# First modulation round in two halves of the features, and the first two SGU tiles begun on the first half

## The chip, the cores and the metric

The kernel runs on one core of a Trainium2 chip, as one program. The metric is the device time of one execution in microseconds (us), shorter is better. The engines are TensorE (PE; PEld is its weight load), VectorE (DVE), ScalarE (ACT), GpSimd (POOL) and SyncE (SP), which mostly issues DMAs. Each engine works through its own instructions in a fixed order and waits on semaphores for the others.

## What is computed

One step of a small hybrid decoder: 1024 prompt tokens and 8 samples of one token each (1032 columns in the kernel), 1024 features. There are two layers. The token mixer of layer 0 is a spatial gating unit (SGU), that of layer 1 sparse attention; a gated ConvGLU follows each. Every sub-layer is modulated by the conditioning vector c:

```python
def ada_params(c, w_ada, b_ada):
    return (jax.nn.silu(c) @ w_ada + b_ada).reshape(c.shape[0], N_MOD, D_MODEL)
def modulate(x, shift, scale):
    return x * (1 + scale[:, None, :]) + shift[:, None, :]
...
        hp = modulate(xp, mp[:, 0], mp[:, 1])
...
def sgu_mixer(h, w_in, b_in, norm_g, norm_b, w_s, b_s, w_out):
    z = jax.nn.gelu(h @ w_in + b_in)
    u, v = jnp.split(z, 2, axis=-1)
```

The change touches only the beginning: shift and scale of layer 0's first sub-layer (the first 2048 of 6144 columns of `w_ada[0]`), `h`, and the first two of sixteen 128-column tiles of `h @ w_in`.

## The kernel before

Activations lie feature-major: a feature tile k (0 to 7) is 128 partitions, the tokens are columns, in three chunks c of 384, 384 and 264 (`CH`; the last 8 columns are the samples). Products are made to float32 accuracy from pieces in a reduced format: every operand is split into a high and a low part, `Hh` and `Hl` for the input, `whi` and `wlo` for the weights, and `mm3` multiplies high by high, high by low and low by high. One `dense` tile is thus 8 x 3 matmuls into one PSUM bank. There are two sets of four banks, `psA` and `psB`.

The start goes like this. `fetch_x` loads rows of x, `turn_x` transposes them on PE and copies them out of PSUM to `R` (ACT for even feature tiles, DVE for odd). `ada_round(0, 0, ...)` loads the first 2048 columns of `w_ada[0]` in eight row blocks k of two 512 KB pieces and multiplies each with silu(c) (L239, L242); its last step copies the sums (L247), transposes them and adds the bias into `MOD` (L255). The bias comes from `PAR`, all small parameters turned feature-major, which `load_params` loads in ten small DMAs (L221) and turns (L228). `affine` makes scales and shifts of `MOD`. `apply` makes `Hh` on ACT (L343), the same in full accuracy as `ht` on DVE (L344), and their difference `Hl` on POOL for even, on DVE for odd feature tiles (L349). `zload` loads one tile of the SGU weights and splits it: on ACT and DVE for tiles 0 and 1 (L101, L106), on POOL for the others (L103, L106). The pool `wp` holds four such parts, so the parts of tile 2 take the place of those of tile 0. `sgu_v(i, c)` is tile i of the gate side over chunk c, with a gelu on ACT (L484); it also scales `R` on POOL (L485).

The order of each engine is not the order of the code: a scheduler of the framework interleaves the instructions by priority and by estimated times when the program is built. DMAs pass through eight completion lanes in turn, over all issuing engines, so the DMA issued as number n waits until number n - 8 has landed. Two steps that belong to later stages were placed into this start by the scheduler: four DMAs that load the page table (L778) and the step of DVE that uses them (L781).

Of the kernel before, what the change touches and what calls it, by code (L numbers as in the profile page):

```python
# [34 lines left out]
# background steps taken per step of the products: indexer, keys and values, queries, attention  # L35
PUMP = (3, 4, 4)
PKV, PQ, PL = 7, 8, 2
# searches for thresholds: which blocks go together on which engine, how many run side by side, steps per step
# [3 lines left out]
# attention: heads in flight by block, units of products ahead of the first block, start of the samples' attention  # L42
# [3 lines left out]
# engines that split the query and output weights  # L46
QE = "GV"
# last feature tiles of each ConvGLU whose down products go by chunks of tokens
KEEP = (3, 4)
# output: columns of the last affine on VectorE, blocks that use the second set of banks  # L50
# [5 lines left out]
def hybrid_step(  # L56
# [51 lines left out]
    def load_w(src, cols, pool=None, eng="GG"):  # L108
        """A [1024, cols] piece of weights, split into two parts."""
# [11 lines left out]
    def load_rows(src, pool=None, eng="GG"):  # L121
        """A [128, 1024] piece of weights."""
# [13 lines left out]
    def load_half(src, j, eng):  # L136
        """Rows 512 j.. of a [1024, 128] piece of weights, both parts in one tile."""
# [46 lines left out]
    def tr(out, in_):  # L184
        PE.transpose(out, in_, ident[:in_.shape[0], :in_.shape[0]])  # L185

    crow = Tt("crow", tag="E")
    SP.dma_start(crow[0:1, :D], c_prompt)
    SP.dma_start(crow[1:9, :D], c_sample)
# [22 lines left out]

    def load_params():
        PROW = Tt("prow", tag="E")
        r = 0
        for src in rows:
            n, s = src.shape[0], 0
            while s < n:
                m = min(n - s, 128 - r % 128)
                i = r // 128  # L220
                SP.dma_start(PROW[r % 128:r % 128 + m, i * 128:(i + 1) * 128], src[s:s + m, :])  # L221
                s += m
                r += m
        b = bank("B")
# [5 lines left out]
    def ada_round(L, r, mk):  # L230
        """w_ada[L][:, 2048 r : 2048 (r+1)] for the nine rows of conditioning, feature-major."""
# [32 lines left out]
    # x, feature-major  # L264
# [22 lines left out]

    win = sgu_w_in[0]
# [11 lines left out]
    # per-feature scales of each sub-layer's input and of its residual  # L300
# [10 lines left out]
    def affine(L, i, lnix):  # L311
        """h = n * G + B and x = n * g + b for n the normalised tokens (or the inputs themselves)."""
# [24 lines left out]
    def apply(c, k, b, af, R, lo="G"):  # L337
        """b: n^T of feature tile k in PSUM (or the inputs), over the tokens of chunk c."""
# [25 lines left out]
    def norm_block(src, j, nt, tag="B"):  # L364
        """Token-major normalised block j; src(k) gives its feature tile k, feature-major."""
# [31 lines left out]
    fetch_x(0)  # L397
    turn_x(0)
    first = ["T"] * 13 + ["P"] * 2 + ["W"]
    steps = ada_round(0, 0, lambda: wp.tile([128, SLOT], F32, name="adaw", tag="W") if first[0] == "W" else Tt("adaw", tag=first.pop(0)))  # L400
    for fn in steps[:8]:
        fn()
    zload(0)
    load_params()
    fetch_x(1)
    fetch_x(2)
    first[:] = ["E"]
    steps[8]()
    af = affine(0, 0, None)

    def first_h(c):
        for k in range(KT):
            apply(c, k, R[c][:, k, :], af, None, "GV"[k % 2])

    first_h(0)
    zload(1)

# [32 lines left out]
    # convolution state of the samples  # L450
# [28 lines left out]
    def sgu_v(i, c):  # L479
        b = dense(pieces[i], 128, c)  # L480
# [4 lines left out]
        G.tensor_scalar(R[c][:, i, :], R[c][:, i, :], ALPHA, 0.0, op0=OP.mult, op1=OP.add)  # L485

    for c in range(3):
        sgu_v(0, c)
        sgu_v(1, c)
        if c < 2:  # L490
            turn_x(c + 1)
            first_h(c + 1)
# [943 lines left out]
```

## Time and profile before

| | |
|---|---|
| median of 3 timed runs | 2643.59 us (2638.25 to 2645.91) |
| profiled execution, span | 2642.5 us (1.1 below that median) |
| PE busy | 2536.9 us, 96% of the span |
| DVE, POOL, ACT busy | 1684.3, 996.0, 793.1 us |
| HBM traffic | 178.41 MB read, 11.27 MB written, 72 GB/s over the span |

The table is read from the top: the span is nearly the timed run, and one engine, PE, fills most of it. The question for any change is then in which stretches PE is not busy, or busy at a lower clock, and what it waits for there. Times of rows count from the span's start.

### The profile page before, as it was taken

Reading aid. Unit: us, or ns where it says so; the run is one execution under the profiler, and the core shown is the slowest. Engines: PE = TensorE matmul, PEld = TensorE weight load, DVE = VectorE, ACT = ScalarE, POOL = GpSimd, SP = SyncE. Lnnn points to the kernel's source line nnn. Section 1 sums busy time; section 2 is a strip of 40 time slices with the busy share of each in tenths; the row PEclk is TensorE's granted clock in tenths of the full one; section 3 lists DMA queues with packets and bytes.
Section 4 is the critical chain, followed back from the end, with each engine's and each line's share of the span. In section 5 each row is a group of like instructions: output and inputs, shape, how many; then the busy total and the mean of one; then the engine's idle time right before and its main releaser. Section 6 shows DMA issues by size and latency. Waiting matters only on the chain.

```text
span 2642.5 us, 40989 instructions
## 1 busy us (share of the span) xinstructions
PE 2536.9 (96%) x15920; PEld 2373.0 (90%) x15920; DVE 1684.3 (64%) x3905; ACT 793.1 (30%) x1610; POOL 996.0 (38%) x1066
## 2 busy tenths in 40 slices
PE   7999999999999999999999989898999999999996
PEld 4898798999999999998887979777999999999996
DVE  3323336677667667755798986434777777777747
ACT  3121224111111111124576876532411111111121
POOL 2433525332222223234245765534523333223335
PEclk8999999999999999999999999998999999999998
DMA  7323402222222222211114112233211111111111
GB/s 274 106 63 106 126 9 72 81 89 80 72 88 87 76 78 91 62 37 50 60 34 117 45 53 64 72 117 108 61 49 48 49 42 44 44 48 48 49 41 66
DMA packets 201928, 192.14 MB, mean 73 GB/s; under 512 B 9806, under 2 KB 178246, under 8 KB 200951
## 3 DMA queue, kind: packets, MB, share of 16 engines
q1 hardware_dynamic: 199047, 180.08, 21.9%
q0 software_dynamic: 2688, 9.44, 1.1%
q8 instruction: 126, 2.06, 0.3%
q14 instruction: 67, 0.55, 0.1%
HBM read 178.41 MB, written 11.27 MB: 72 GB/s over the span
## 4 chain that ended last, share of the span: by engine, by line
PE 77%; DVE 10%; POOL 4%; DMA 4%; ACT 3%; issue 3%; SPq 0%; ACTq 0%; POOLq 0%; DVEq 0%
PE psA L84 48%; PE psB L84 21%; PE psB L185 3%; DVE Cc L655 3%; PE psB L242 2%; DVE R L575 1%; ACT junk L920 1%; PE psA L185 1%; DVE junk L889 1%; DVE S L869 1%; DMA raw<-in_dsa_w_out_dram 1%; DMA adaw<-in_w_ada_dram 1%; DVE R L579 1%; POOL whi L103 1%; DMA pidx<-in_page_table_dram 0%
## 5 line engine op out<-in xcount | busy, mean ns | idle before, releaser
L84 PE MATMUL psA<-Hh,whi 128*128 128x384 f32 (+1 forms) x2912 | 940.2, 324 | 17.3 <-POOL whi L103 8.6
L84 PE MATMUL psA<-Hl,whi 128*128 128x384 f32 (+1 forms) x2912 | 938.5, 322 | 1.0 <-POOL Hl L349 0.7
L84 PE MATMUL psA<-Hh,wlo 128*128 128x384 f32 (+1 forms) x2912 | 936.1, 322 | 1.8 <-DVE wlo L106 1.8
L575 DVE SCALAR_TENSOR_TENSOR R<-psB,g,R 128x384 f32<-128x384 f32 (+1 forms) x952 | 525.6, 568 | 299.1 <-PE psB L84 296.9
L103 POOL TENSOR_SCALAR whi<-raw 128x1024 fp32r<-128x1024 f32 x179 | 194.1, 1084 | 1111.3 <-PE psA L84 978.9
L84 PEld LDWEIGHTS psA<-Hh,whi 128*128 128x128 f32 x2912 | 551.8, 190 | 45.7 <-issue 20.7
L84 PEld LDWEIGHTS psA<-Hl,whi 128*128 128x128 f32 x2912 | 552.6, 190 | 9.8 <-issue 6.7
L84 PEld LDWEIGHTS psA<-Hh,wlo 128*128 128x128 f32 x2912 | 552.1, 190 | 8.0 <-issue 5.0
L106 POOL TENSOR_TENSOR wlo<-raw,whi 128x1024 fp32r<-128x1024 f32 x163 | 402.5, 2469 | 12.7
L84 PE MATMUL psB<-gh,whi 128*128 128x384 f32 (+1 forms) x1056 | 342.7, 325 | 6.0 <-DVE t L578 3.0
L84 PE MATMUL psB<-gh,wlo 128*128 128x384 f32 (+1 forms) x1056 | 338.2, 320 | 0.0
L84 PE MATMUL psB<-gl,whi 128*128 128x384 f32 (+1 forms) x1056 | 337.9, 320 | 0.0
L655 DVE SCALAR_TENSOR_TENSOR Cc<-As,PAR,Cc 128x256 f32<-128x256 f32 (+3 forms) x264 | 270.4, 1024 | 54.9 <-ACT Cc L650 53.7
L84 PEld LDWEIGHTS psB<-gh,whi 128*128 128x128 f32 x1056 | 198.6, 188 | 29.7 <-issue 15.3
L84 PEld LDWEIGHTS psB<-gl,whi 128*128 128x128 f32 x1056 | 198.7, 188 | 0.0
L84 PEld LDWEIGHTS psB<-gh,wlo 128*128 128x128 f32 x1056 | 198.5, 188 | 0.0
L101 ACT ACTIVATE gh<-Cc 128x384 fp32r<-128x384 f32 x132 | 65.0, 492 | 432.7 <-DVE Cc L662 432.7
L657 ACT ACTIVATE Cc<-Cc 128x384 f32<-128x384 f32 x132 | 64.9, 492 | 402.1 <-DVE Cc L655 402.1
L649 ACT ACTIVATE As<-psA 128x384 f32<-128x384 f32 x132 | 60.4, 458 | 342.4 <-PE psA L84 342.4
L84 PE MATMUL psB<-Hh,wh 128*128 128x384 f32 (+1 forms) x512 | 136.2, 336 | 3.2 <-ACT R L351 1.1
L662 DVE TENSOR_TENSOR Cc<-psA,Cc 128x384 f32<-128x384 f32 x132 | 67.7, 513 | 107.6 <-PE psA L84 107.1
L579 DVE TENSOR_TENSOR R<-R,t 128x8 f32<-128x8 f32 x328 | 131.0, 406 | 2.9
(352 smaller groups left out, 3284.1 us busy)
## 6 DMA issues: line engine op xcount, KB each, us to landing
raw<-in_ffn_w_up_dram SPq DMA_DIRECT2D x88, 512.0 KB
raw<-in_w_ada_dram SPq DMA_DIRECT2D x64, 512.0 KB
raw<-in_ffn_w_down_dram SPq DMA_DIRECT2D x44, 512.0 KB
adaw<-in_w_ada_dram SPq DMA_DIRECT2D x32, 512.0 KB
raw<-in_sgu_w_in_dram SPq DMA_DIRECT2D x16, 512.0 KB
raw<-in_dsa_w_in_dram SPq DMA_DIRECT2D x16, 512.0 KB
raw<-in_dsa_w_out_dram SPq DMA_DIRECT2D x32, 256.0 KB
raw<-in_sgu_w_out_dram SPq DMA_DIRECT2D x8, 512.0 KB
```

The costliest lines, as they stand in the source:

```text
L84: PE.matmul(out, l, r, start=start, stop=stop)
L101: A.activation(hi, src, AF.Copy)
L103: G.tensor_scalar(hi, src, 1.0, 0.0, op0=OP.mult, op1=OP.add)
L106: (V if e_lo == "V" else G).tensor_tensor(lo, src, f(hi), op=OP.subtract)
L185: PE.transpose(out, in_, ident[:in_.shape[0], :in_.shape[0]])
L242: PE.matmul(st["b"][32 * g:32 * g + 32, :512], SCT[:, k, :], rw[g // 2][:, (g % 2) * 512:(g % 2 + 1) * 512], start=(k == 0), stop=(k == KT ...
L575: V.scalar_tensor_tensor(R[c][:, dt, :npr], b[:, :npr], gp[:, dt:dt + 1], R[c][:, dt, :npr], op0=OP.mult, op1=OP.add)
L579: V.tensor_tensor(R[c][:, dt, npr:n], R[c][:, dt, npr:n], t8, op=OP.add)
L649: A.activation(As[:, c0:c0 + n], b[:, :n], AF.Copy)
L655: V.scalar_tensor_tensor(Cc[:, a0:c0 + npr], As[:, a0 - d:c0 + npr - d], w, Cc[:, a0:c0 + npr], op0=OP.mult, op1=OP.add)
L657: A.activation(Cc[:, c0:c0 + n], Cc[:, c0:c0 + n], AF.Gelu_apprx_tanh)
L662: V.tensor_tensor(Cc[:, c0:c0 + n], b[:, :n], Cc[:, c0:c0 + n], op=OP.mult)
```

## The change

The first modulation round is loaded in two halves: half 0 holds features 0 to 511 of shift and of scale, half 1 the others. A piece is still 512 KB, now 128 rows of two runs of 512 floats. Half 0 (eight pieces) is loaded and multiplied, and feature tiles 0 to 3 of `h` are made for all three chunks, after all of x has been turned. Then SGU tiles 0 and 1 run over feature tiles 0 to 3 of each chunk into six open banks (`zb`), with the eight products of half 1 in between. Then `MOD` gets half 1, feature tiles 4 to 7 of `h` follow, and the six sums are finished. The conditioning rows and the small parameters are issued by ACT, not by SP. Comment lines were taken out.

```diff
     crow = Tt("crow", tag="E")
-    SP.dma_start(crow[0:1, :D], c_prompt)
-    SP.dma_start(crow[1:9, :D], c_sample)
+    A.dma_start(crow[0:1, :D], c_prompt)
+    A.dma_start(crow[1:9, :D], c_sample)
...
+    PROW = Tt("prow", tag="E")
     def load_params():
-        PROW = Tt("prow", tag="E")
...
-                SP.dma_start(PROW[r % 128:r % 128 + m, i * 128:(i + 1) * 128], src[s:s + m, :])
+                A.dma_start(PROW[r % 128:r % 128 + m, i * 128:(i + 1) * 128], src[s:s + m, :])
...
+    def turn_params():
         b = bank("B")
...
+    def half_load(k, hh):
+        w = Tt("adaw", tag="P" if k in (2, 5) else "T")
+        SP.dma_start(w[:, :1024].rearrange("p (s c) -> p s c", s=2),
+                     w_ada[0, k * 128:(k + 1) * 128, :2048].rearrange("p (s c) -> p s c", s=2)[:, :, 512 * hh:512 * hh + 512])
+        return w
+    def half_step(k, w, b):
+        for g in range(4):
+            PE.matmul(b[32 * g:32 * g + 32, :256], SCT[:, k, :], w[:, 256 * g:256 * g + 256], start=(k == 0), stop=(k == KT - 1),
+                      skip_group_check=True)
+    def half_end(hh, b):
+        S = Tt("adas")
+        A.activation(S[:, :256], b[:, :256], AF.Copy)
+        b2 = bank("B")
+        for j in range(2):
+            tr(b2[:, j * 128:(j + 1) * 128], S[:, j * 128:(j + 1) * 128])
...
+        for j in range(2):
+            for i in range(2):
+                V.tensor_tensor(mo[:, j, i], src[:, j, i, :, 0:9], bb[:, j, i].unsqueeze(2).to_broadcast([128, 2, 9]), op=OP.add)
...
-    fetch_x(0)
-    turn_x(0)
-    first = ["T"] * 13 + ["P"] * 2 + ["W"]
-    steps = ada_round(0, 0, lambda: wp.tile([128, SLOT], F32, name="adaw", tag="W") if first[0] == "W" else Tt("adaw", tag=first.pop(0)))
-    for fn in steps[:8]:
-        fn()
-    zload(0)
-    load_params()
-    fetch_x(1)
-    fetch_x(2)
-    first[:] = ["E"]
-    steps[8]()
-    af = affine(0, 0, None)
-    def first_h(c):
-        for k in range(KT):
-            apply(c, k, R[c][:, k, :], af, None, "GV"[k % 2])
-    first_h(0)
-    zload(1)
+    load_params()
+    fetch_x(0)
+    aw = [[half_load(k, 0) for k in range(KT)]]
+    zload(0)
+    fetch_x(1)
+    zload(1)
+    fetch_x(2)
+    turn_x(0)
+    turn_params()
+    b = bank("B")
+    for k in range(KT):
+        half_step(k, aw[0][k], b)
+    aw.append([half_load(k, 1) for k in range(KT)])
+    half_end(0, b)
...
+    def first_h(c, hh):
+        for k in range(4 * hh, 4 * hh + 4):
+            apply(c, k, R[c][:, k, :], (*af0, None, None), None, "GV"[k % 2])
+    first_affine(0)
+    for c in range(3):
+        if c:
+            turn_x(c)
+        first_h(c, 0)
...
-    def sgu_v(i, c):
-        b = dense(pieces[i], 128, c)
+    def sgu_v(i, c, b=None):
+        b = dense(pieces[i], 128, c) if b is None else b
...
+    zb = {(i, c): bank("B" if c == 2 else "A") for c in range(3) for i in range(2)}
+    def z_half(i, c, hh):
+        c0, n = CH[c]
+        for k in range(4 * hh, 4 * hh + 4):
+            mm3(zb[i, c][:, :n], (pieces[i][0][:, k, :], pieces[i][1][:, k, :]), (Hh[:, k, c0:c0 + n], Hl[:, k, c0:c0 + n]),
+                k == 0, k == KT - 1)
+    b = bank("B")
+    left = deque(range(KT))
+    for n, (i, c) in enumerate((i, c) for c in range(3) for i in range(2)):
+        z_half(i, c, 0)
+        for _ in range(1 if n < 4 else 2):
+            k = left.popleft()
+            half_step(k, aw[1][k], b)
+    half_end(1, b)
+    first_affine(1)
     for c in range(3):
-        sgu_v(0, c)
-        sgu_v(1, c)
-        if c < 2:
-            turn_x(c + 1)
-            first_h(c + 1)
+        first_h(c, 1)
+        for i in range(2):
+            z_half(i, c, 1)
+            sgu_v(i, c, zb[i, c])
```

The order of SP's queue at the start, before; `raw` of x_prompt is x chunk 0, `xt` chunks 1 and 2, `raw` of sgu_w_in a weight tile, `prow` the small parameters:

```order
L275 DMA raw<-in_x_prompt_dram 128x1024 x3
L239 DMA adaw<-in_w_ada_dram 128x1024 x16
L221 DMA prow<-in_ln_g_dram 32x128
L221 DMA prow<-in_ln_b_dram 32x128
L221 DMA prow<-in_b_ada_dram 64x128
L112 DMA raw<-in_sgu_w_in_dram 128x8x128
```

The same place in the changed kernel:

```order
L278 DMA raw<-in_x_prompt_dram 128x1024 x3
L294 DMA adaw<-in_w_ada_dram 128x2x512 x8
L278 DMA xt<-in_x_prompt_dram 128x1024 x5
L278 DMA xt<-in_x_sample_dram 8x1024
L294 DMA adaw<-in_w_ada_dram 128x2x512
L112 DMA raw<-in_sgu_w_in_dram 128x8x128 x2
L294 DMA adaw<-in_w_ada_dram 128x2x512 x7
L112 DMA raw<-in_sgu_w_in_dram 128x8x128
L485 DMA w_726<-in_sgu_w_s_dram 8x8x1
L515 DMA out_dram<-in_state_conv_dram 8x2816 x2
L837 DMA pidx<-in_page_table_dram 32x8x1 x4
```

Eight pieces of the modulation weights now stand ahead of chunks 1 and 2 of x, and eight behind; the page table still stands behind all of them and three weight tiles.

DVE's queue before, from the low part of weight tile 1 to the first inputs of chunk 1; `D` is a small constant, `R_105` chunk 1 of x:

```order
L106 TENSOR_TENSOR wlo<-raw,whi 128x1024
L447 TENSOR_TENSOR D_313<-ident,w_690 8x64
L781 TENSOR_SCALAR pidx<-pidx,iop 128x8
L284 COPY R_105<-psA 128x384
L344 TENSOR_SCALAR ht<-R_105,Gp,Bp 128x384 x2
L349 TENSOR_TENSOR Hl<-ht,Hh 128x384
```

DVE's queue in the changed kernel, from the last inputs of the first half to the first of the second (`af` are the scales and shifts, `R_105` is here chunk 0):

```order
L377 TENSOR_TENSOR Hl<-ht,Hh 128x264
L487 TENSOR_TENSOR D_417<-ident,w_726 8x64
L840 TENSOR_SCALAR pidx<-pidx,iop 128x8
L314 TENSOR_TENSOR MOD_101<-psB,PAR 128x2x9 x4
L444 COPY af_268<-MOD_101 128x4
L446 COPY af_270<-MOD_101 128x32
L443 TENSOR_SCALAR af_267<-MOD_101 128x4
L445 TENSOR_SCALAR af_269<-MOD_101 128x32
L372 TENSOR_SCALAR ht<-R_105,af_267,af_268 128x384 x2
```

The step that waits for the page table stood ahead of chunk 1's inputs, and now stands ahead of the second half's sums.

## Rows read from the trace of the kernel before

**Rows 1.** The head of the page, and busy time, share and instructions by engine
```profile
span 2642.5 us, 40989 instructions
...
PE 2536.9 (96%) x15920; PEld 2373.0 (90%) x15920; DVE 1684.3 (64%) x3905; ACT 793.1 (30%) x1610; POOL 996.0 (38%) x1066
```

**Rows 2.** Windows: start:end, length, each engine's busy time, granted clock, DMA share, GB/s
```profile
0.00:30.00 30.00, 21.40 (x96) 7.25 (x96) 2.82 (x8) 4.24 (x6) 1.38 (x17) 1.00 0.93 352
35.00:48.00 13.00, 11.18 (x32) 9.16 (x33) 9.35 (x13) 6.45 (x11) 9.46 (x12) 0.50 0.72 230
39.00:43.00 4.00, 3.86 (x12) 3.14 (x11) 3.75 (x6) 0.20 (x1) 4.00 (x6) 0.50 1.15 303
48.00:52.00 4.00, 4.00 (x24) 3.96 (x24) 0.00 (x0) 0.00 (x0) 0.00 (x0) 1.00 0.05 0
52.00:61.00 9.00, 3.35 (x17) 2.71 (x16) 4.31 (x9) 4.53 (x8) 2.35 (x3) 0.66 0.90 282
61.00:82.00 21.00, 20.69 (x133) 18.75 (x132) 18.20 (x50) 11.54 (x24) 14.91 (x23) 0.98 0.16 48
82.00:1200.00 1118.00, 1105.80 (x6921) 1033.06 (x6920) 645.95 (x1379) 220.70 (x442) 364.70 (x260) 1.00 0.25 78
1200.00:1900.00 700.00, 649.15 (x4131) 583.30 (x4130) 486.27 (x1374) 407.11 (x834) 355.59 (x588) 0.96 0.24 72
```

**Rows 3.** Timeline of SP's DMA issues: start, length, engine, line, tile
```profile
9.67 0.33 SPq L239 DMA_DIRECT2D adaw<-in_w_ada_dram  x1
...
19.95 0.33 SPq L221 DMA_DIRECT2D prow<-in_ln_g_dram  x1
```

**Rows 4.** Timeline from the last modulation product to the first activation
```profile
29.12 1.05 PE L242 MATMUL psB<-adaw,SCT 128*32 128x512 f32 x4 [0.47 <-DMA adaw<-in_w_ada_dram]
...
30.28 0.60 ACT L247 ACTIVATE adaw<-psB 128x512 f32<-128x512 f32 x1 [18.70 <-PE psB L242]
...
32.79 0.48 ACT L228 ACTIVATE PAR<-psB 128x368 f32<-128x368 f32 x1 [0.68 <-PE psB L185]
...
34.30 1.90 ACT L343 ACTIVATE Hh<-R,Bp,Gp 128x384 fp32r<-128x384 f32 x3 [1.03 <-DVE Gs L320]
```

**Rows 5.** Groups by line and form, 30 to 82 us: busy, mean ns, idle before
```profile
L284 DVE COPY R<-psA 128x384 f32<-128x384 f32 x4 | 2.2, 550 | 0.7 <-PE psA L185 0.7
...
L106 DVE TENSOR_TENSOR wlo<-raw,whi 128x1024 fp32r<-128x1024 f32 x2 | 2.6, 1286 | 19.6 <-ACT whi L101 19.6
```

**Rows 6.** Timeline of PE, first SGU products
```profile
44.38 0.69 PE L84 MATMUL psA<-Hh,whi 128*128 128x384 f32 x1 [1.09 <-ACT whi L101]
...
62.16 0.34 PE L84 MATMUL psA<-Hh,whi 128*128 128x384 f32 x1
62.33 0.34 PE L84 MATMUL psA<-Hl,whi 128*128 128x384 f32 x1
```

**Rows 7.** Chain of waits, 34 to 56 us, and the step of DVE behind it
```profile
34.23 9.02 DMA raw<-in_sgu_w_in_dram
...
43.27 12.18 DMA pidx<-in_page_table_dram
...
55.58 0.23 DVE L781 TENSOR_SCALAR pidx<-pidx,iop 128x8 int32<-128x8 int32 x1 [9.74 <-DMA pidx<-in_page_table_dram]
```

**Rows 8.** Timeline of DVE, inputs of the SGU products
```profile
62.29 0.67 DVE L349 TENSOR_TENSOR Hl<-ht,Hh 128x384 fp32r<-128x384 f32 x1
...
64.64 0.66 DVE L349 TENSOR_TENSOR Hl<-ht,Hh 128x384 fp32r<-128x384 f32 x1
...
75.08 0.40 DVE L344 TENSOR_SCALAR ht<-R,Gp,Bp 128x256 f32<-128x256 f32 x1
...
79.74 0.87 DVE L349 TENSOR_TENSOR Hl<-ht,Hh 128x264 fp32r<-128x264 f32 x1
```

**Rows 9.** Timeline of POOL and PE at the end of the first two tiles
```profile
81.23 1.05 POOL L103 TENSOR_SCALAR whi<-raw 128x1024 fp32r<-128x1024 f32 x1 [0.91 <-PE psA L84]
...
81.71 1.88 PE L84 MATMUL psB<-wsT,ones 128*128 128x512 f32 x4
```

More of the change, by code (lines that the diff above doesn't have):

```diff
@@ L286, in turn_x @@
                 A.activation(R[c][:, k, :], b[:, :CH[c][1]], AF.Copy)
+    def half_load(k, hh):
[13 more added lines that the diff above has]
+            tr(b2[:, j * 128:(j + 1) * 128], S[:, j * 128:(j + 1) * 128])
+        bb = PAR[:, pBADA:pBADA + 16].rearrange("p (s h g j) -> p h j s g", s=2, h=2, g=2)[:, hh]
+        mo = MOD[0][:, 0:16, :].rearrange("p (s h g j) c -> p h j s g c", s=2, h=2, g=2)[:, hh]
+        src = b2[:, :256].rearrange("p (j s g c) -> p j s g c", j=2, s=2, g=2)
+        for j in range(2):
+            for i in range(2):
+                V.tensor_tensor(mo[:, j, i], src[:, j, i, :, 0:9], bb[:, j, i].unsqueeze(2).to_broadcast([128, 2, 9]), op=OP.add)
     win = sgu_w_in[0]
@@ L394, in ln_steps, with first_affine @@
         return out
+    load_params()
     fetch_x(0)
-    turn_x(0)
-    first = ["T"] * 13 + ["P"] * 2 + ["W"]
-    steps = ada_round(0, 0, lambda: wp.tile([128, SLOT], F32, name="adaw", tag="W") if first[0] == "W" else Tt("adaw", tag=first.pop(0)))
-    for fn in steps[:8]:
-        fn()
-    zload(0)
-    load_params()
-    fetch_x(1)
-    fetch_x(2)
-    first[:] = ["E"]
-    steps[8]()
-    af = affine(0, 0, None)
-    def first_h(c):
-        for k in range(KT):
-            apply(c, k, R[c][:, k, :], af, None, "GV"[k % 2])
-    first_h(0)
-    zload(1)
+    aw = [[half_load(k, 0) for k in range(KT)]]
[3 more added lines that the diff above has]
+    fetch_x(2)
+    turn_x(0)
+    turn_params()
[4 more added lines that the diff above has]
+    half_end(0, b)
+    af0 = [sm.tile([128, KT] + ([NB] if i > 1 else []), F32, name=f"af0{i}", tag=t) for i, t in enumerate(("Gp", "Bp", "Gs", "Bs"))]
+    def first_affine(hh):
+        k = slice(4 * hh, 4 * hh + 4)
+        V.tensor_scalar(af0[0][:, k], mod(0, 1)[:, k, 0], 1.0, None, op0=OP.add)
+        V.tensor_copy(af0[1][:, k], mod(0, 0)[:, k, 0])
+        V.tensor_scalar(af0[2][:, k], mod(0, 1)[:, k, 1:9], 1.0, None, op0=OP.add)
+        V.tensor_copy(af0[3][:, k], mod(0, 0)[:, k, 1:9])
+    def first_h(c, hh):
[6 more added lines that the diff above has]
+        first_h(c, 0)
     wsT = Tt("wsT")
@@ L484, in sgu_v @@
         A.activation(VT[i][:, c0:c0 + n], b[:, :n], AF.Gelu_apprx_tanh, bias=PAR[:, pSBI + 8 + i:pSBI + 9 + i])
-        G.tensor_scalar(R[c][:, i, :], R[c][:, i, :], ALPHA, 0.0, op0=OP.mult, op1=OP.add)
-    for c in range(3):
-        sgu_v(0, c)
-        sgu_v(1, c)
-        if c < 2:
-            turn_x(c + 1)
-            first_h(c + 1)
+        if i > 1:
+            for k in ([i] if i < 6 else [i, i - 6]):
+                G.tensor_scalar(R[c][:, k, :], R[c][:, k, :], ALPHA, 0.0, op0=OP.mult, op1=OP.add)
+    zb = {(i, c): bank("B" if c == 2 else "A") for c in range(3) for i in range(2)}
[13 more added lines that the diff above has]
+    first_affine(1)
+    for c in range(3):
+        first_h(c, 1)
+        for i in range(2):
+            z_half(i, c, 1)
+            sgu_v(i, c, zb[i, c])
     zload(2)
```

## Prediction

> **What bounds the kernel now.** The first view is the page's head: PE is busy 2536.9 of 2642.5 us [rows 1], so only the 105.6 us in which it is not can be won without taking work away. The busy time by stretches says where these lie [rows 2]. In the first 61 us PE idles 8.6, 1.8 and 5.7 us in the stretches 0 to 30, 35 to 48 and 52 to 61, and it also runs 35 to 48 us and part of 52 to 61 us at half the clock (granted 0.50 and 0.66); from 82 to 1200 us it idles only 12 us in 1118; from 1200 to 1900 us, the stage of searches and attention, 50.9 us. The change lies in the first stretch. What that stretch waits for is read from the timeline. The pieces of the first modulation round, 512 KB each, land every (19.95 - 9.67) / 8 = 1.285 us (an issue by SP marks the landing of the load eight places earlier [rows 3]), until the last products start at 29.12; then follow the copy of the sums (30.28), the copy of the parameters (32.79) and the first scaled activations (34.30) [rows 4]. From there the products of SGU tile 0 run behind DVE and POOL, and the chain shows two more loads in a row: weights until 43.27, and the page table's four loads, 12.18 us, until 55.45 [rows 7]. DVE stands in line behind that table (its row at 55.58 waited 9.7 us), and with it the chunk-1 inputs that PE needs. The early stage is over when PE starts the sums for the gating constants at 81.71, and the second SGU weight pair follows at once [rows 9]. I use that point as the mark, and ask when the changed kernel reaches it.
>
> **The change, part by part.** No product is removed: the same 144 products for SGU tiles 0 and 1, the same transposes, the same bytes. What changes is what stands ahead of what.
>
> First half of the modulation. Eight 512 KB loads go ahead instead of sixteen. Their runs are 2 KB long where they were 4 KB, which no row shows. The bounds are the 4 KB rows (1.285 us) and the 512-byte runs of the SGU weights, 0.524 MB at the 303 GB/s of 39 to 43 us = 1.73 us [rows 2]; I take 1.3, near the first since 2 KB is half of 4 KB but four times 512 B. With the first landing at 9.67 as before, the eighth lands at 9.67 + 7 x 1.3 = 18.8 (bounds 18.7 and 21.8), against 28.9. The Trainium skill (DMA: Bandwidth & Descriptors, Why small descriptors are slow) counts a fixed overhead of some three cycles for each packet; by its figures 4 KB in two packets takes about 2% more than in one, an estimate of 0.4 us over the sixteen loads, and the sum by that would be 0.2 us shorter than with 1.3.
>
> The twelve small loads now issued by ACT are queued ahead of its first copies of x. Each waits for a load eight places earlier; by the landings above ACT is through at about 13.5 us. Its four copies of x chunk 0 then end at 15.5, still ahead of 18.8: no cost. If they were 5 us later it would cost 2.
>
> From the last half-load to the first activation. 18.8, plus four 256-column products (half of 1.05 [rows 4]) 0.55, the copy 0.45, transposes of two blocks of sums, of x block 3 (which lands one load later) and of the last parameters 1.1: the parameter copy starts at 20.9; from there to the first activation took 34.30 - 32.79 = 1.5 [rows 4], so 22.4.
>
> Until the first product. PE must now turn all of chunks 1 and 2 first, and the low weight part of tile 0 stands on DVE behind four pairs of feature tiles (a pair took 64.64 - 62.29 = 2.35 [rows 8]) and six copies of x at 0.55 or less [rows 5], some 2.6 us with overlap: 22.4 + 9.4 + 2.6 = 34.4, plus 1.29 for that part [rows 5] = 35.7. The first products start on the high part a little earlier; I take 35.5. Both weight pieces land at 18.8 + 6 x 1.3 + 2 x 1.73 = 30.1, hidden by this. So products begin about where they began before, right behind the activation at 34.30 [rows 4]; the gain must come behind this point, where chunk 1 and 2 inputs are now ready and PE need not wait.
>
> The half products on PE: 48 of 384 columns at 62.33 - 62.16 = 0.17 [rows 6], 24 of 264 at 0.12, seven half-steps of the second modulation half at 0.53: 8.3 + 2.9 + 3.7 = 14.9. PE has only short transposes from 20 to 35 us, so it starts at the half clock; before, the clock rose 3.9 us after PE had begun to run without a gap at 44.38 [rows 2, 6], so 1.9 us are lost. End: 35.5 + 14.9 + 1.9 = 52.3; with copy and transposes 53.1.
>
> The second half then waits for two things on DVE. One is that end, 53.1. The other is the page table: its step now stands right ahead of the second half's sums. The loads queued ahead of the table are 18.8 + 5 x 1.3 + 1.3 + 2 x 1.73 + 7 x 1.3 + 1.73 = 40.9, and the table took 12.18 [rows 7]: 53.1 too. Neither hides the other by more than a fraction; bounds 50 and 58.
>
> From there: sums and scales 0.9, then activations at 54.2. Four pairs of chunks 0 and 1 at 2.35 are 9.4; the last two pairs of chunk 2 took 75.08 to 80.61 (79.74 + 0.87), 5.5 [rows 8], of which 0.8 were copies of x now done earlier: 4.7. DVE ends at 68.3. PE ended 1.1 after DVE (80.61 to 81.71 [rows 8, 9]): 69.4. PE itself, 11.2 us of products and 1.1 of transposes from 54.9 with 2 us lost to the clock, would end at 69.2, so DVE sets it by a little.
>
> **Sum.** 81.7 - 69.4 = 12.3 us earlier at the mark. What follows is bound by PE: the weights of tile 2 are split when tile 0 lets their buffer go, at 81.23 before, half a us ahead of the mark [rows 9], and so again. Behind the mark, of some 15,000 PE rows 538 stand elsewhere, most of them in the stage of 1200 to 1900 us; I take that at nothing, bounds 4 us each way from 50.9 us of idle there. Span 2642.5 - 12.3 = 2630.2; the median of the timed runs is 1.1 above the profiled span, so **2631.3**.
>
> **Rivals.**
> A. The table or the second half is late, by about 6 us (58 to 59 instead of 53): the table's packets might wait behind more, or the half products start late. For it: everything from 40 us on hangs on a single load on one queue, and DVE has nothing behind it. Against: the bytes ahead of it are the same as before. 2637.
> B. The second half runs at the half clock throughout. Then 72 products take 2 x 11.2, and PE ends at 54.9 + 22.4 + 1.1 = 78.4, a gain of 3.3: 2640. For it: PE waits from 52.3 to 54.9, and from 35 to 48 us the clock did stay at 0.50 while PE waited for each input [rows 2]. Against: two tiles a pair give PE 12 x 0.35 = 4.2 us of slow work for each 2.35 us of input, so it has no gaps, and rose 3.9 us after the gaps ended. The Trainium skill (TensorE: Matmul & The Clock Gate, Part 1) has the array fall to the low level after an idle stretch and come back only with sustained work; it speaks against cutting a stream of products in two with a wait between, and by it the wait would cost the 2 us that the sum holds, not this rival's 9.
> C. The gain is larger: DVE is freed from POOL's traffic and the pairs run at 2.0, or the table is done by 50: 4 to 5 us more, 2627.
> D. Nothing at the mark: the order of engines that the program now fixes makes chunk 1 and 2 copies and the weight split late, products start at 45. Then all is 10 us later: 2641. Against: each piece of that path is in rows 4, 5 and 8.
> E. Slower: the reordered pieces in the stage of 1200 to 1900 us bring a new wait between searches and attention. PE idles 50.9 us there [rows 2]; to end at 2652 or more, 20 us would have to be added, 40% of it. For it: that stage has the most engines in turn. Against: few rows moved, and by small distances.
>
> **Chances.** My forecast 0.55 (its own range 2627 to 2635), A 0.12, B 0.07, C 0.13, D 0.08, E 0.05. A change under 0.3% (7.9 us, below 2651.5 and above 2635.7) is what a measurement of this kernel can't tell from none. The forecast and C are faster but for a twelfth of them (0.62), and a third of A (0.04); A's rest, B and D are within; E is slower, with 0.02 for mishaps of size. Faster 0.66, same 0.27, slower 0.07. The range, leaving out E and the tails of C and D: 2624 to 2641.
>
> **What would show it.** In the changed profile: the eighth half-load lands near 18.8 (its products wait for it at 18.5 to 19.5); first activation at 22 to 23; first SGU product at 34 to 37, at granted clock 0.50; the wait of DVE for the table ends at 52 to 55, and the sums of the second half stand within 1 us behind it; the gating constants' sums start at 68 to 71. From there on each stage is as long as before to 1%. The prediction is wrong if products start after 40, if the table lands after 58, if the granted clock is still 0.50 beyond 62 us, or if PE's idle time from 1200 to 1900 us moves by over 5 us.

## The result and the profile after

The changed kernel takes 2628.85 us (median of 4 runs, 2626.55 to 2629.34) against 2640.92 us of before in the same comparison: ratio 0.9947, 95% interval 0.993 to 0.9965, so 12 us or 0.5% faster. It was timed twice more, with ratios 0.9959 (0.9943 to 0.9974) and 0.9962 (0.9947 to 0.9976). The number on record, 2631.3, and its range hold. The way to it was half wrong: by the repeats below, the start gives about half of those 12 us, and the rest comes behind it, mostly behind 1200 us, where I had forecast nothing.

The head of the page after, beside [rows 1]: PE does the same work, in 64 more instructions, and has the same share.

```profile
span 2624.8 us, 41121 instructions
...
PE 2525.8 (96%) x15984; PEld 2369.4 (90%) x15984; DVE 1676.1 (64%) x3913; ACT 793.2 (30%) x1611; POOL 998.4 (38%) x1066
```

The stretches of after, in the columns of [rows 2]:

```profile
0.00:30.00 30.00, 19.01 (x125) 12.07 (x125) 8.86 (x27) 10.72 (x19) 5.91 (x23) 0.84 0.98 339
24.00:35.00 11.00, 7.94 (x36) 4.94 (x35) 10.25 (x20) 8.90 (x17) 8.23 (x11) 0.50 1.08 346
35.00:48.00 13.00, 13.00 (x69) 10.24 (x70) 8.55 (x24) 2.78 (x6) 3.94 (x8) 0.77 0.60 199
48.00:52.00 4.00, 4.00 (x34) 3.20 (x36) 0.23 (x1) 0.00 (x0) 0.00 (x0) 1.00 0.53 144
52.00:61.00 9.00, 6.89 (x54) 4.77 (x50) 3.87 (x14) 4.09 (x8) 2.92 (x4) 0.84 0.97 305
61.00:82.00 21.00, 19.20 (x108) 16.88 (x107) 18.14 (x37) 8.67 (x15) 17.69 (x20) 0.99 0.12 34
82.00:1200.00 1118.00, 1107.55 (x6956) 1035.77 (x6955) 647.09 (x1381) 223.06 (x445) 360.39 (x262) 1.00 0.25 78
1200.00:1900.00 700.00, 649.19 (x4163) 586.12 (x4162) 489.23 (x1388) 407.89 (x836) 362.38 (x587) 0.96 0.24 74
```

From 35 to 48 us PE now has no gap (13.00 of 13.00, before 11.18) and does 69 matmuls in place of 32 (transposes and half-steps among them); from 52 to 61 us it does 54 in place of 17. The page table's load is still there, but PE works across it. From 1200 to 1900 us PE idles 50.8 us, as before (50.9).

Before, the first product of the tiles stood at 35.06:

```profile
35.06 0.69 PE L84 MATMUL psA<-Hh,whi 128*128 128x384 f32 x1 [2.30 <-ACT Hh L343]
```

The timeline of after, three engines, from the last first-half products to the mark:

```profile
19.91 0.64 PE L300 MATMUL psB<-adaw,SCT 128*32 128x256 f32 x8 [0.45 <-DMA adaw<-in_w_ada_dram]
...
22.81 0.48 ACT L231 ACTIVATE PAR<-psB 128x368 f32<-128x368 f32 x1 [1.82 <-PE psB L185]
24.22 2.50 ACT L371 ACTIVATE Hh<-R,af,af 128x384 fp32r<-128x384 f32 x4 [0.93 <-DVE af L445]
...
32.57 5.81 PE L185 MATMUL psA<-ident,xt 128*128 128x128 f32 x21
...
35.48 1.32 DVE L106 TENSOR_TENSOR wlo<-raw,whi 128x1024 fp32r<-128x1024 f32 x1
...
38.31 0.69 PE L84 MATMUL psA<-Hh,whi 128*128 128x384 f32 x1
...
51.67 0.23 DVE L840 TENSOR_SCALAR pidx<-pidx,iop 128x8 int32<-128x8 int32 x1 [7.38 <-DMA pidx<-in_page_table_dram]
...
56.56 0.43 DVE L314 TENSOR_TENSOR MOD<-psB,PAR 128x18 f32<-128x18 f32 x4 [4.66 <-PE psB L185]
57.30 6.87 ACT L371 ACTIVATE Hh<-R,af,af 128x384 fp32r<-128x384 f32 x12 [1.27 <-DVE af L443]
...
66.95 0.48 DVE L372 TENSOR_SCALAR ht<-R,af,af 128x256 f32<-128x256 f32 x1
...
73.10 0.87 DVE L377 TENSOR_TENSOR Hl<-ht,Hh 128x264 fp32r<-128x264 f32 x1
...
75.24 1.88 PE L84 MATMUL psB<-wsT,ones 128*128 128x512 f32 x4
```

DVE still waits 7.38 us for the table, but the wait ends at 51.67, and what stands behind it, the second half's sums, could not run before 56.56 anyway, since they wait 4.66 us more for PE. The wait of [rows 7] is covered. The mark of [rows 9] moves from 81.71 to 75.24.

To see where the rest comes from I use a second mark, one step of DVE that each kernel has once, ahead of the indexer. Before and after:

```profile
1227.98 0.51 DVE L753 TENSOR_SCALAR misc<-misc 128x128 f32<-128x128 f32 x1
```

```profile
1217.48 0.51 DVE L812 TENSOR_SCALAR misc<-misc 128x128 f32<-128x128 f32 x1
```

In this pair of profiles the lead is 6.5 us at the mark, 10.5 at the second mark and 17.7 at the end (2642.5 - 2624.8). One pair is not enough to explain 5 us, as the repeats show.

### The profile page after: what moved, and what is told of

It is laid out like the page before. It is cut to its first block, busy times and chain, and to the rows that moved or that the text cites. A ratio compares the mean times of both kernels' runs of the same rounds, so it can differ in the third digit from the quotient of the medians.

```text
span 2624.8 us, 41121 instructions
## 1 busy us (share of the span) xinstructions
PE 2525.8 (96%) x15984; PEld 2369.4 (90%) x15984; DVE 1676.1 (64%) x3913; ACT 793.2 (30%) x1611; POOL 998.4 (38%) x1066
## 4 chain that ended last, share of the span: by engine, by line
PE 80%; DVE 11%; POOL 3%; issue 2%; ACT 2%; DMA 2%; ACTq 0%; SPq 0%; POOLq 0%; DVEq 0%
PE psA L84 50%; PE psB L84 23%; PE psB L185 3%; PE psB L245 2%; DVE Cc L714 2%; DVE junk L948 1%; DVE R L634 1%; PE psA L185 1%; ACT junk L979 1%; DVE S L928 1%; POOL L L1252 0%; DMA raw<-in_dsa_w_out_dram 0%; DMA adaw<-in_w_ada_dram 0%; DVE R L638 0%; PE psA L1308 0%
## 5 line engine op out<-in xcount | busy, mean ns | idle before, releaser
L714 DVE SCALAR_TENSOR_TENSOR Cc<-As,PAR,Cc 128x256 f32<-128x256 f32 (+3 forms) x264 | 262.2, 993 | 56.1 <-ACT Cc L709 54.9
```

Of the source, the lines that this page charges most:

```text
L714: V.scalar_tensor_tensor(Cc[:, a0:c0 + npr], As[:, a0 - d:c0 + npr - d], w, Cc[:, a0:c0 + npr], op0=OP.mult, op1=OP.add)
```

## The experiments

Theory A: the halves bring the start forward by themselves. Theory B: all they give is cover for the table's wait. C: the table's packets slow what runs beside them. L: a table step that stands late costs time in the indexer stage. O: the later stage is written in another order, and that is worth some us. S (scatter): the half-clock stretches fall differently in each execution. "Lead" is the time of a mark in the first profile of before minus that in the profile named; "gain" is the median of before in the same comparison minus that of the kernel. In three kernels (e_after_pt2, e_after_sp, e_after_warm) PE splits the four products of the mark, and the first two count; the other two start 2.2 to 3.0 us later there (at 76.57, 84.18 and 81.78), so these three marks flatter their kernels.

| kernel | mark | lead there | second mark | lead there | median us | gain | ratio, 95% interval |
|---|---|---|---|---|---|---|---|
| before | 81.71 | | 1227.98 | | | | |
| e_before_again | 82.16 | -0.5 | 1225.53 | 2.5 | 2639.87 | -1.3 | 1.0003 (0.999 to 1.0016) |
| after | 75.24 | 6.5 | 1217.48 | 10.5 | 2628.85 | 12.1 | 0.9947 (0.993 to 0.9965) |
| e_after_again | 77.65 | 4.1 | 1221.33 | 6.7 | 2630.5 | 12.0 | 0.9959 (0.9943 to 0.9974) |
| e_after_third | 76.94 | 4.8 | 1221.40 | 6.6 | 2628.63 | 10.0 | 0.9962 (0.9947 to 0.9976) |
| e_before_pt | 72.66 | 9.1 | 1218.52 | 9.5 | 2657.31 | -14.9 | 1.0066 (1.0048 to 1.0083) |
| e_after_pt | 73.73 | 8.0 | 1218.10 | 9.9 | 2652.86 | -10.4 | 1.0048 (1.0032 to 1.0065) |
| e_before_pt2 | 75.32 | 6.4 | 1222.54 | 5.4 | 2631.69 | 8.3 | 0.9971 (0.996 to 0.9982) |
| e_after_pt2 | 73.76 | 8.0 | 1219.97 | 8.0 | 2637.9 | 2.1 | 0.9996 (0.9987 to 1.0005) |
| e_before_act | 79.91 | 1.8 | 1226.49 | 1.5 | 2641.05 | 1.4 | 0.9993 (0.9981 to 1.0006) |
| e_after_sp | 81.18 | 0.5 | 1229.30 | -1.3 | 2644.01 | -4.0 | 1.0017 (1.0008 to 1.0027) |
| e_after_warm | 79.59 | 2.1 | 1226.71 | 1.3 | 2643.7 | -3.7 | 1.0016 (1.0006 to 1.0025) |
| e_after_pt2_sp | 76.55 | 5.2 | 1221.74 | 6.2 | 2639.81 | -0.1 | 0.9997 (0.9986 to 1.0007) |
| e_before_pt2_act | 72.57 | 9.1 | 1217.60 | 10.4 | 2633.48 | 6.3 | 0.9969 (0.9957 to 0.9981) |

### What the wait for the table is worth

**The table as 32 numbers, step in a later stage** (e_before_pt, e_after_pt). One DMA of 32 numbers in place of four that write 32 partitions each; one product with a 4 x 128 selector spreads them.

```diff
+    gsel = sm.tile([128, 384], F32, name="gsel", tag="ht", bufs=2)[0:4, 0:128]
+    SP.dma_start(ptI, bass.AP(tensor=page_table.tensor, offset=page_table.offset, ap=[[1, 4], [4, 8]]), allow_slow_non_contiguous=True)
...
+    mm(b[:, :8], gsel, ptF, True, True)
     for g in range(4):
-        SP.dma_start(pidx[32 * g:32 * g + 32, :], bass.AP(tensor=page_table.tensor, offset=page_table.offset + g, ap=[[0, 32], [4, 8]]),
...
-    V.tensor_scalar(pidx, pidx, 32.0, iop, op0=OP.mult, op1=OP.add)
+    V.tensor_scalar(pidx, b[:, :8], 32.0, iop, op0=OP.mult, op1=OP.add)
```

> The kernel before, but the page table is read as 32 numbers (one small DMA) and spread over the partitions by one small product in a later stage, so that DVE no longer waits for it between SGU products. Mark: the start of the sums for the gating constants, 81.71 us before, 75.24 in the changed kernel. Theory A (the halves give the gain, since inputs and products begin on half of the modulation): without the table's wait the old order still has to make chunks 1 and 2 behind chunk 0, mark at 77 to 79, time 3 to 5 us below before. Theory B (the gain is only that the changed kernel covers the table's wait with products): mark at 75.5 or earlier, time as short as the changed kernel's or shorter.

> The changed kernel with the same small read of the page table. In its trace the table had landed (DVE's step at 51.67) 4.9 us before the second half's sums could start (56.56). Theory A and B both expect no change at the mark: 75.2 within 0.5. Theory C (the table's packets slow the loads and steps around them as well): mark 1 to 3 us earlier.

Taking away the wait alone gives before a mark of 72.66, 9.1 us earlier and earlier than any profile of the changed kernel: B holds at the mark, A doesn't. The time that B forecast did not come: both kernels are slower than before, since the product now stands late in PE's queue. The same edit moves the changed kernel's mark to 73.73, 1.5 to 3.9 us ahead of its three profiles, which C asked for; but the clock of the start was another in this profile (shown under the clock of PE), so C is not shown.

The form of the load costs the 12 us, and not its place in the queue: the one load of e_before_pt is issued at the place of the four, and POOL has it 3.2 us later. The timeline of e_before_pt, SP, POOL, PE and DVE:

```profile
42.12 0.46 SPq L779 DMA_DIRECT2D ptI<-in_page_table_dram  x1
...
45.32 0.19 POOL L780 TENSOR_SCALAR ptF<-ptI 4x8 f32<-4x8 int32 x1 [1.30 <-DMA ptI<-in_page_table_dram]
...
1246.96 0.30 POOL L782 TENSOR_SCALAR_AFFINE_SELECT gsel<-gsel 4x128 f32<-4x128 f32 x1
...
1247.31 0.59 PE L84 MATMUL psB<-ptF,gsel 4*128 4x8 f32 x2 [3.23 <-POOL gsel L782]
...
1247.94 0.23 DVE L788 TENSOR_SCALAR pidx<-psB,iop 128x8 int32<-128x8 f32 x1 [2.54 <-PE psB L84]
```

Windows of e_before_pt, and of before:

```profile
1220.00:1300.00 80.00, 65.44 (x346) 57.67 (x347) 37.98 (x130) 38.59 (x71) 32.15 (x49) 0.81 0.20 71
```

```profile
1220.00:1300.00 80.00, 75.41 (x477) 69.76 (x476) 51.89 (x206) 47.90 (x89) 38.42 (x56) 0.96 0.24 81
```

PE does 346 products there in place of 477, with 14.6 us idle in place of 4.6 and at granted clock 0.81: it waits for the selector behind POOL's queue, and work that filled this stretch before is written behind it.

**The same, with the step in the start** (e_before_pt2, e_after_pt2). The selector sits in free columns of `prow`, the product beside the transposes of the small parameters, the DVE step behind it.

```diff
+        gsel = PROW[0:4, 512:640]
...
+        PE.matmul(b[:, 384:392], gsel, ptF, start=True, stop=True)
         A.activation(PAR, b[:, :NPAR], AF.Copy)
+        V.tensor_scalar(pidx, b[:, 384:392], 32.0, iop, op0=OP.mult, op1=OP.add)
```

> Before, with the page table read as 32 numbers by one small DMA and spread over the partitions by one product, this time beside the small parameters: DVE's step stands in the start, not in the indexer's stage. The computation is unchanged. Theory B (all that the halves give is cover for the table's 9.7 us wait on DVE, and a lead at the mark carries to the end): mark at 72 to 74.5, and a time of 2629 to 2635, 8 to 11 below before and within 4 of the changed kernel. Theory A (halves bring a gain of their own behind the mark, by the order that the program now fixes): mark the same, but the time stays 6 or more above the changed kernel, 2636 to 2641. Theory L (the late place of the step and of the gathers cost the two earlier page-table kernels their 20 us between 1267 and 1368 us): a lead of 8 to 11 at 1267 us that is still there to 3 us at 1368.

> The changed kernel with the same early page-table step; the small load is issued by ACT with the other small ones. The computation is unchanged. Theory B: with the long wait gone the halves have nothing left to cover; mark at 72.5 to 75, time 2626 to 2633, no better than the same edit of before (within 3). Theory A: 5 or more better than the same edit of before, 2621 to 2627. Theory L: the lead at 1267 us is still there at 1368.

In e_before_pt2 DVE's step now waits a quarter of a us; the start is otherwise laid out as in before. Its timeline:

```profile
33.74 0.23 DVE L242 TENSOR_SCALAR pidx<-psB,iop 128x8 int32<-128x8 f32 x1 [0.27 <-ACT PAR L241]
...
75.32 1.88 PE L84 MATMUL psB<-wsT,ones 128*128 128x512 f32 x4
```

The mark, 0.8 later than B had it, equals that of the changed kernel's first profile, and the gain is 8.3 us against its 10.0 to 12.1, with a few lines and no halves. L holds too: the lead of 5.4 at the second mark is not lost in the stage that cost the first version 20 us. The first gather that uses the table starts at 1381.5 there, 7.0 us ahead of before (1388.5), and in e_before_pt at 1398.6, 10.1 us behind it. With the wait gone, the halves have nothing left to give: without the wait the marks are 72.66 and 75.32 in one piece, 73.73 and 73.76 in halves, and e_after_pt2 has a worse time. So B is shown for the start, though not its times for e_after_pt2: 2637.9 is above what B (2626 to 2633) and A (2621 to 2627) had. That time, 6 us worse than the lead of 8.0 would give, belongs to the open question below.

### The small loads

e_before_act makes this part of the change alone (modulation in one piece); e_after_sp takes it back from the changed kernel.

```diff
-    A.dma_start(crow[0:1, :D], c_prompt)
+    SP.dma_start(crow[0:1, :D], c_prompt)
...
-                A.dma_start(PROW[r % 128:r % 128 + m, i * 128:(i + 1) * 128], src[s:s + m, :])
+                SP.dma_start(PROW[r % 128:r % 128 + m, i * 128:(i + 1) * 128], src[s:s + m, :])
```

> One part of the change alone: conditioning rows and small parameters issued by ACT ahead of everything, modulation still in one piece. Its order from the indexer on is nearly that of the changed kernel. At the mark: the last parameters no longer hold up the loads and the first activation, so chunk 0 starts 2 to 3 us earlier; the page table still stands on DVE; mark at 79 to 80. Behind the mark: if the changed order of the later stages gives the part of the gain that does not stand at the mark (theory O), this kernel gains 5 us or more behind its mark as well; if that part is scatter of the clock from one execution to the next (theory S), its lead over before moves by up to 3 us either way.

> The changed kernel with the conditioning rows and the small parameters issued by SP again, ahead of x; twelve small loads then stand ahead of the first half-load. The computation is unchanged. If the small loads only cost their queue time (0.33 us or so each on SP, and a lane each): half-loads land 2 to 4 us later, mark 1 to 4 later than the changed kernel's two profiles (75.2 and 77.7), time 2629 to 2634. Rival: the mark hangs on the chain from the table's load and the second half, not on the first half-loads: mark unchanged within 1.5, time 2627 to 2631.

Alone it is worth nothing that can be measured: 1.8 us at the mark, as expected, and none of the 5 us behind it that O asked for. In the changed kernel it is needed. The timeline of e_after_sp, SP, PE, DVE and PE:

```profile
7.51 6.49 SPq L294 DMA_DIRECT2D adaw<-in_w_ada_dram  x8
...
23.95 0.64 PE L300 MATMUL psB<-adaw,SCT 128*32 128x256 f32 x8 [0.72 <-DMA adaw<-in_w_ada_dram]
...
63.00 0.43 DVE L314 TENSOR_TENSOR MOD<-psB,PAR 128x18 f32<-128x18 f32 x4 [8.75 <-PE psB L185]
...
81.18 1.95 PE L84 MATMUL psB<-wsT,ones 128*128 128x512 f32 x2
```

The last first-half products start 4.0 us later (19.91 to 23.95), the second half's sums 6.4 later, the mark 5.9 later than in the first profile of after and 3.5 later than in the latest of the three. The table is not at fault (its step stood at 54.02, 9 us ahead of the sums), so the rival in the expectation falls: the start hangs on the first half-loads. The whole gain is gone, but not at the mark alone: the time is 10 us above what was expected, and the gain some 15 us below the changed kernel's (-4.0 against 11.4 us). What lies behind the mark is part of the open question below.

### The clock of PE in the start

Products that nobody reads are put behind each half-step of the first half and each feature tile of chunks 1 and 2 of x, to keep PE busy. Those behind the half-steps write, with `start=True`, to other columns of the bank in which the sums are still open. Contrary to the expectation this kernel's outputs are not those of the change, so only its trace and time are read.

```diff
         half_step(k, aw[0][k], b)
+        for _ in range(3):
+            PE.matmul(b[:, 256:384], ident, ident, start=True, stop=True, skip_group_check=True)
```

> The changed kernel with products that nobody reads: three 128-column ones behind each of the eight half-steps of the first half, and three behind each feature tile of chunks 1 and 2 of x, so that PE has less idle time from 15 to 33 us. The outputs are unchanged. If the granted clock of 0.50 from 20.5 to 41.0 is what made the first half late (my term was 1.9 us, the trace shows the 21 transposes at 32.57 taking 5.81 us): the clock stays at 1.00 or comes back by 34, first product at 35 to 37 instead of 38.3, mark 2 to 4 earlier than 75.2 to 77.7. Rival: the first products wait for DVE's low parts and inputs, not for PE's speed, or the added products stand in PE's way as much as the clock gives: first product at 38 to 40, mark within 1.5.

Windows of e_after_warm, to read against 24 to 35 us and 35 to 48 us of after, and one row of its timeline:

```profile
24.00:35.00 11.00, 11.00 (x105) 9.58 (x97) 7.31 (x22) 7.37 (x14) 5.04 (x7) 1.00 1.08 347
35.00:48.00 13.00, 13.00 (x96) 9.84 (x94) 12.53 (x30) 5.62 (x10) 8.33 (x12) 1.00 0.59 192
```

```profile
61.87 0.43 DVE L316 TENSOR_TENSOR MOD<-psB,PAR 128x18 f32<-128x18 f32 x4 [9.06 <-PE psB L185]
```

The clock stays at 1.00 (2.4 GHz) where after had 0.50 (1.2 GHz) and 0.77. But PE is now busy without a gap, and the added products stand in the way for longer than the clock gives back: the first product of the tiles starts at 45.85 in place of 38.31, and the second half's sums at 61.87 in place of 56.56. That is the rival's reason, but later than either side expected (38 to 40, mark within 1.5).

What a higher clock is worth there without added work, e_after_pt shows by chance: its edit touches the start only in the table's load and step, and its granted clock from 24 to 35 us was 0.78. Its timeline of PE, the same 21 transposes and the first product:

```profile
30.48 2.78 PE L185 MATMUL psA<-ident,xt 128*128 128x128 f32 x15
33.93 1.11 PE L185 MATMUL psA<-ident,xt 128*128 128x128 f32 x6 [0.68 <-DVE R L287]
34.98 0.45 PE L84 MATMUL psA<-Hh,whi 128*128 128x384 f32 x1
```

The 21 transposes take 3.89 us in place of 5.81, the first product starts 3.3 us earlier (0.6 of this stood already at the last half-load, whose products start at 19.30), and the second half's sums 3.0 earlier, at 53.53.

### What happens behind the second mark

Two kernels that differ from the page-table ones in the queue of the small loads. In the stage from 1200 us on, e_after_pt2_sp is written nearly as after and e_before_pt2, and e_before_pt2_act word for word as e_before_act.

```diff
-    A.dma_start(ptI, bass.AP(tensor=page_table.tensor, offset=page_table.offset, ap=[[1, 4], [4, 8]]), allow_slow_non_contiguous=True)
+    SP.dma_start(ptI, bass.AP(tensor=page_table.tensor, offset=page_table.offset, ap=[[1, 4], [4, 8]]), allow_slow_non_contiguous=True)
```

> The changed kernel with the early page-table step, the one small table load issued by SP where it was issued by ACT. The start is the same but for that one issue; in the indexer, search and attention stage (1200 to 1900 us) the scheduler now writes nearly the order that the changed kernel and the early-table version of before have (DVE differs from these in 18 and 4 rows of that stage, from its ACT twin in 126). The computation is unchanged. Theory O (the order written for the later stage is worth +2 to +5 us in these two and -5 in the ACT twin, whatever the start is): lead over before of 7 to 9 at 1170 us and 10 to 13 at 1920; time 2626 to 2631, 7 or more below the ACT twin's 2637.9. Theory S (the later differences are scatter of one execution): lead at 1920 about that at 1170, time 2633 to 2640.

> Before with the early page-table step, and with all small loads issued by ACT ahead of x: the edits of two kernels that gained 8.3 us and 1.4 us. The computation is unchanged. Its order in the later stage is word for word that of the kernel with the small loads alone (0 rows of PE and of DVE differ), which lost 2.6 us there. Theory O: lead at 120 us 7 to 9 (6.4 and 1.8 added), lead at 1920 us 2 to 5 below the lead at 1170; time 2632 to 2637, later than the early table alone in spite of the earlier start. Theory S or plain sums: lead kept to 1.5, time 2627 to 2631.

O meets a kernel that it doesn't fit. With nearly the order that is fast elsewhere (what the few rows do that differ was not tested), e_after_pt2_sp has a lead of 6.2 at the second mark and gains nothing in time. e_before_pt2_act adds two edits and its leads do add up (9.1 at the mark, 10.4 at the second), the best start of all, but its time is no better than that of e_before_pt2; that part is what O asked for, and alone it proves nothing.

**Repeats** (no edit).

> The changed kernel once more, for a second profile and five more rounds. Theory S (scatter): mark at 75.2 within 0.3, since the start is fixed, but the lead over before at 1200 us and at the end differs from the first profile's (10.4 and 17.7 us) by 2 to 5 us. Theory O (order): both within 1 us of it.

> The kernel before, once more, for its own scatter. Theory S (the chip's half-clock stretches fall where they like in each execution): mark 81.7 within 3, and its lead over the first profile of before wanders by 2 to 5 us between 120 and 1920; the stretch of half clock at 1871 us may be missing. Theory R (what the profiles show behind 120 us belongs to the kernel): lead 0 within 1 throughout, the stretch at 1871 us is there again. Time 2637 to 2643.

> The changed kernel a third time. Theory S: lead over the first profile of before 4 to 7 at 120 us, and at 1920 us anything from 5 to 15; the two earlier profiles had 15.1 and 8.9. Theory R: lead grows from 1170 to 1920 us by 2 to 5 as in both earlier profiles, and no half-clock stretch stands between 1855 and 1885 us. Time 2626 to 2632.

The same program scatters by 2.4 us at the mark (75.24, 77.65, 76.94; the expectation had 0.3), by 3.9 at the second mark, and by 8.6 at the end (2624.8, 2631.8, 2633.4). The repeats ran on two different chips, so what chips differ by is in this too. At the mark the scatter has a place: DVE ends its last inputs at 73.97, 74.76 and 74.15, within 0.8 us, but the mark follows by 1.3, 2.9 and 2.8 us. Windows of after, e_after_again and e_after_third:

```profile
74.00:76.00 2.00, 2.00 (x14) 1.62 (x13) 0.17 (x1) 1.80 (x4) 1.15 (x2) 1.00 0.00 0
```

```profile
74.00:76.00 2.00, 2.00 (x11) 2.00 (x10) 0.93 (x2) 0.60 (x1) 0.47 (x1) 0.50 0.03 8
```

```profile
74.00:76.00 2.00, 2.00 (x11) 2.00 (x11) 0.31 (x2) 1.07 (x2) 0.00 (x0) 0.50 0.00 0
```

In both repeats PE did its last products at half clock. It had waited 1.29 us for DVE just before; in after it had waited 1.28 us there, and the clock stayed. Further behind, an example is a half-clock stretch near 1870 us, here in windows of before, after and e_after_third:

```profile
1870.00:1880.00 10.00, 10.00 (x51) 8.91 (x51) 8.12 (x26) 5.37 (x11) 5.54 (x7) 0.66 0.17 54
```

```profile
1860.00:1870.00 10.00, 10.00 (x71) 9.63 (x71) 9.62 (x24) 4.83 (x11) 7.73 (x8) 1.00 0.15 54
```

```profile
1865.00:1875.00 10.00, 10.00 (x51) 9.06 (x50) 7.44 (x24) 4.30 (x9) 6.45 (x8) 0.67 0.15 54
```

Two profiles of after lack it, the third has it, 51 products in 10 us in place of 71; both of before have it. From the first pair of profiles I would have told this as a part of the gain.

So S explains much of what single profiles show, but not all. Against the mean of the two profiles of before at the second mark (1226.8), the three of after lead by 9.3, 5.4 and 5.4, on average 6.7; the three timed gains are 12.1, 12.0 and 10.0, on average 11.4. Some 4 to 5 us thus come behind 1220 us. The same sum gives 8.3 - 4.2 = +4.1 for e_before_pt2, but -2.9 for e_before_pt2_act, -4.7 for e_after_pt2 and -5.1 for e_after_pt2_sp. Each of these carries the scatter of one profile, 2 to 4 us, and of the timed interval, 0.1% or 2.6 us; from +4 to -5 is more than either. The written order sorts these but for e_after_pt2_sp, so O isn't shown, and one kernel stands against it.

Within the profiles themselves, the stretch from the second mark to the end took 1414.5 and 1419.4 us in the two of before, 1407.3, 1410.5 and 1412.0 in the three of after. The windows of that stretch, before and after:

```profile
1227.98:2642.50 1414.52, 1342.66 (x8509) 1271.88 (x8509) 980.12 (x2370) 529.01 (x1097) 592.48 (x735) 0.97 0.20 61
```

```profile
1217.48:2624.80 1407.32, 1336.26 (x8509) 1269.46 (x8509) 970.16 (x2371) 529.74 (x1097) 595.03 (x735) 0.97 0.20 61
```

The same 8509 matmuls keep PE busy for 1342.7 and 1346.9 us in the profiles of before, for 1336.3, 1336.0 and 1339.5 in those of after, while its idle time is 71.1 to 74.5 us in all five. So the gain there is not idle time. The granted clock, 0.97 in four of them and 0.98 in one, doesn't sort it either. What decides those 5 us either way is open.

## Why the prediction was right, and where it wasn't

**Mechanism.** Right: products start 3 us behind where they began (38.31, before 35.06), and the gain is made behind, by covering the table's wait. e_before_pt2 shows that this wait is the whole of the start's gain.

**First half.** Forecast 18.8 for the eighth landing, 20.9 for the parameter copy, 22.4 for the first activation; measured 19.91 (products that wait for it), 22.81 and 24.22. The landing itself was 1.1 late, which no run explains; the transposes behind it were costed at full clock. (The estimate for 4 KB in two packets has its sign wrong: 0.4 us over sixteen loads makes the sum 0.2 longer than with 1.3 us each, not shorter.) Twelve small loads on ACT: no cost, right, since ACT is through at 12.63; e_after_sp shows their place was worth 3.5 to 5.9 us at the mark.

**First product.** Forecast 35.5, measured 38.31. The wrong step was the "low weight part of tile 0" on DVE as the limit. DVE had that part at 36.80 (35.48 + 1.32, forecast 35.7), but PE was still turning x: its last 21 transposes take 5.81 us, 0.28 each, and end at 38.38. From 24 to 35 us its granted clock was 0.50, which I had put into the sum for the products alone (1.9 us). In e_after_pt, at 0.78, the first product stood at 34.98. My reading that the clock stayed at 0.50 before because "PE waited for each input" is too simple: from 39 to 43 us PE was busy 3.86 of 4.00 us and stayed at 0.50 [rows 2].

**Half products.** Forecast 16.8 from first product to end, measured 55.58 - 38.31 = 17.3. Right. The table's step stands 1.4 before the forecast 53.1, at 51.67, and is covered by 4.9 us, not by "a fraction". The sums start at 56.56, 3.5 behind that forecast: of rival A (some 6 late) half came, by the late first product and not by the table.

**Second half.** From its activations (57.30) the four pairs end at 66.95, 9.65 against 9.4. The last two pairs take until 73.97 (73.10 + 0.87) where I had 4.7: 7.0. That term was mis-sized: I had taken the rows of chunk 2 and deducted copies. DVE's small steps are longer here (last section), and POOL works beside more of it (17.69 of the 21 us from 61 on, before 14.91 [rows 2]); that this is the reason was not tested.

**Sum.** Forecast mark 69.4, measured 75.24: +2.8 for the first product, +0.5 for the products, -0.2 up to the activations, +2.6 for the pairs (2.3 of it the last two), +0.2 behind DVE. In the repeats PE at half clock adds some 1.6 more behind DVE. The gain at the mark is 4 to 6.5 us, not 12.3.

**Behind the mark.** "I take that at nothing, bounds 4 us each way" failed: by the repeats some 6 us come there (11.4 less 5.3, the mean lead at the mark over both profiles of before), 4 to 5 of them behind the second mark, and the cause is open. PE's idle time from 1200 to 1900 us didn't move (50.8 against 50.9; 54.0 and 52.3 in the repeats), so the sign that I had named for it would not have shown it. At the mark the forecast had 7 us too much, behind it 6 too little; the two cancel. That the number came within 3 us is luck, not the working.

**Signs.** Of what was to show it, few came as written. Late or early by 0.3 to 4.2 us were the eighth half-load (19.91), the first activation (24.22), the first product (38.31), the end of the table's wait (51.67) and the gating constants' sums (75.24); the second half's sums stood 4.9 us behind the table and not 1. Right were the first product's clock of 0.50 and the later stages, as long as before to 1%. Of the signs of being wrong, one came in the repeats: their clock was still 0.50 beyond 62 us.

**Rivals.** B (half clock through the second half) came in part. In after, products took 0.52 us until 61.5 and 0.34 from there, and PE kept the full clock to the mark. In the repeats the clock was back at about 63.5 and 62.6 and fell once more at about 73, so that there PE and not DVE set the mark. The Trainium skill (TensorE: Matmul & The Clock Gate, Part 1) has the array come back with sustained work after an idle stretch, and the trace agrees: PE waited until 58.05, then worked on, and from 61.5 the clock was back. C didn't come: a pair still took 2.4 us. Of D a small part came, since products started late, at 38.31 and not at 45. E didn't come for this kernel, but e_before_pt is just that: a step written late between queues, 15 us slower.

## What to carry to other kernels

Before work is rearranged to cover a wait, ask what it is a wait for: here 32 numbers, fetched in a form that took 12.18 us [rows 7], and one smaller load with one product gave three quarters of the gain (8.3 of 11.4 us; 6.3 in the kernel that also moved the small loads). A step made cheap must also stay where its inputs are ready: the same product, placed late, cost 15 us. And with differences of 0.5%, take at least two profiles of either kernel before a stretch is named as the place of the gain.

## What the runs showed of the hardware

Four loads that spread 32 numbers of 4 bytes over 128 partitions took 12.18 us [rows 7], and from 48 to 52 us nothing else moved (0 GB/s [rows 2]). One load of the same 32 numbers to four partitions, issued at the same place, was there 3.2 us later (e_before_pt).

DVE's short steps can be four times as long. The two additions of 128x8 took 0.28 us in before at 78.96. In all three profiles of after they took 1.15, beside a POOL step of the same length; that POOL was the cause was not tested. The timeline of after:

```profile
71.46 1.15 DVE L375 TENSOR_TENSOR ht<-ht,af 128x8 f32<-128x8 f32 x2
71.48 1.11 POOL L468 TENSOR_SCALAR_AFFINE_SELECT ws<-ws 128x1024 f32<-128x1024 f32 x1
```

The runs also show what the granted clock is worth in the start. From 24 to 35 us, where PE waits on and off, it was 0.50, 0.50 and 0.55 in the three profiles of after and 0.78 in e_after_pt; PE filled with work ran at 1.00 there. The 21 transposes took 0.28 us each at 0.50, and 15 of them 0.19 each in e_after_pt, at 1.00.
